# Layer modulation of a two-layer diffusion trunk: contraction summed on VectorE, partitions summed on TensorE, one block of 512 columns at a time

## The chip, the core and the metric

The kernel is one program on one core of one Trainium2 chip. The metric is device time in microseconds (us). The engines are named as in the profile: PE is TensorE, PEld its weight loads, DVE is VectorE, ACT is ScalarE, POOL is GpSimd, and SP issues the DMAs. Each engine works through its own instructions in a fixed order.

## The reference, cut to what matters

The model is a trunk of two layers with 512 latent and 256 context tokens and width 1024. In each layer the token mixer and the ConvFFN are modulated by six vectors (shift, scale, gate, twice), which come from a conditioning vector for each stream:

```python
silu_c, silu_cc = jax.nn.silu(c), jax.nn.silu(c_ctx)          # 1 x 1024 each
mod_x = split(silu_c  @ ada_w[l] + ada_b[l], 6)               # ada_w[l]: 1024 x 6144, latent stream
mod_c = split(silu_cc @ ada_w[l] + ada_b[l], 6)               # context stream
o_ctx, o_lat = token_mixer(modulate(h_ctx, mod_c[0], mod_c[1]), modulate(h_lat, mod_x[0], mod_x[1]), ...)
new_lat = post_norm(h_lat, mod_x[2] * o_lat, ...)
f_lat   = conv_ffn(modulate(new_lat, mod_x[3], mod_x[4]), ...)
new_lat = post_norm(new_lat, mod_x[5] * f_lat, ...)
```

The token mixer has four branches (retention, latent attention, SSD, LRU). Each branch's output is multiplied by its branch matrix, weighted by the sigmoid of a gate projection, and the four are summed.

## The kernel before, in words

All fp32 products are made of three matmuls on a high and a low part (lines 220 to 222 are such a triple). A weight tile of 128x1024 arrives by DMA from SP into `wr`; ACT rounds it to `wh` (line 205), and DVE makes the remainder `wl` in two subtractions of 128x512 (line 143, called from line 209). These three are rings of a few slots.

In each layer the mixer is one long chain, written branch by branch, and behind it a queue of *merge units* (the function `merge`), 8 for each branch, 32 in a layer. A unit multiplies a gate column (24 matmuls on the 512 latent tokens and, in layer 0, 24 on the 256 context tokens) and a branch column (12 and 12). ACT takes the tanh of the gate (line 1442), and DVE multiplies with the branch product: `s<-s,g` of 128x512, then of 128x256 (both by the helper on line 152). A unit after the first branch adds the earlier sum, a 128x768 or two smaller additions on line 143. The function `weave` places these units between the steps of the chain: each step of the chain brings a credit, each unit says by its `yield` what credit it uses up, and units are drawn while there is credit. So a unit is PE work that fills the places where the chain would leave PE idle. A scheduler then fixes the order of each engine's instructions before the run, by the order of writing, by raised priorities (weights are brought forward) and by its own estimates.

Each modulation vector is two blocks of 512 columns, so there are 12 blocks in a layer. The four that the first layer's start needs are made ahead. The other 20 are made by the generator `ada_all` in five groups of four blocks: 20 steps, one behind each of the first 20 merge units of layer 0. A step loads four tiles of 512 KB of `ada_w`, straight into `wh` and `wl` slots. Eight matmuls (line 349) have 32 columns of the conditioning vector `silu` as weights, and write 32 rows each, so that four blocks stand side by side in one PSUM tile `g`. ACT or DVE (lines 351, 353) then adds that to the group's sum `r`. At the end of a group that needs column vectors (three of the five; `MODV`) four matmuls with `sel` (line 358) turn them, and the helper `ada_col` adds the bias on DVE into `modc`. The other two groups load the bias by DMA (line 366), add it, and store rows to DRAM (line 370).

Of the kernel before, what the change touches and what calls it, by code (L numbers as in the profile page):

```python
# [8 lines left out]
F32 = mybir.dt.float32  # L9
# [7 lines left out]
P = 128  # L17
# [51 lines left out]
ADA_R = 'hlhl'  # L69
# [29 lines left out]
def trunk(tc, xin, cc, const, pv, pr, rows, ada_b, ada_w, w_in, w_uq, w_ukv, w_lg, w_br, w_out, w_up, w_dn, out):  # L99
# [3 lines left out]
    def nm(p):  # L103
        uid[0] += 1
        return f"{p}{uid[0]}"
# [3 lines left out]
    with ExitStack() as ctx:  # L109
        E = ctx.enter_context  # L110
        cp = E(tc.tile_pool(name="cp", bufs=1))
# [6 lines left out]
        dp = E(tc.tile_pool(name="dp", bufs=1, space=DRAM))  # L118
# [3 lines left out]
        act, dve, pool, pe, sy = nc.scalar, nc.vector, nc.gpsimd, nc.tensor, nc.sync  # L122

        def S(dt=F32, w=T):
            return cur[-1].tile([P, w], dt, tag="q" if w == 512 and len(cur) == 2 else "s", name=nm("s"), **({"bufs": N_HALF} if w == 512 and len(cur) == 2 else {}))

        def G():
            return pg.tile([P, 512], F32, tag="g", name=nm("g"))

        def C():  # L130
            return pc.tile([P, 512], F32, tag="c", name=nm("c"))

        def small(n, tag="sm", dt=F32):
            return sm.tile([P, n], dt, tag=tag, name=nm(tag))

        def T256(dt=F32, tag="t"):
            return tp.tile([P, 256], dt, tag=tag, name=nm("t"), bufs=N_T if tag == "t" else N_V)
# [4 lines left out]
        def tt(o, a, b, op):  # L142
            dve.tensor_tensor(out=o, in0=a, in1=b, op=op)  # L143

        def ts(o, a, s1, op0, s2=None, op1=None):
            if s2 is None:
                dve.tensor_scalar(out=o, in0=a, scalar1=s1, scalar2=None, op0=op0)
            else:
                dve.tensor_scalar(out=o, in0=a, scalar1=s1, scalar2=s2, op0=op0, op1=op1)

        def stt(o, a, s, b, op0, op1, total=None):
            dve.scalar_tensor_tensor(out=o, in0=a, scalar=s, in1=b, op0=op0, op1=op1, accum_out=total)  # L152

        MUL, ADD, SUB, MAX, MIN = ALU.mult, ALU.add, ALU.subtract, ALU.max, ALU.min
# [38 lines left out]
        def W4(tag, n, dt=F32R):  # L193
            return wp.tile([P, 1024], dt, tag=tag, name=nm(tag), bufs=n)

        def whole(ap, f=1024, tag="wr"):
            t = W4(tag, {"wr": N_WR, "wh": N_WH, "wl": N_WL}[tag], F32)
            sy.dma_start(out=t[:, 0:f], in_=ap[:, 0:f])
            return t
# [110 lines left out]
        modr = [dp.tile([2, 2, 2, 512], F32, name=f"modr{l}") for l in range(DEPTH)]  # L310
        sel = cp.tile([P, 10], F32, name="sel")
        sy.dma_start(out=sel, in_=const[:, _CO["sel"][0]:_CO["sel"][0] + 10])
        MODV = {0: 0, 1: 1, 3: 2, 4: 3}
# [13 lines left out]
        def ada_col(l, b, src, n):  # L327

            vec, half = b // 2, b % 2
            c0 = 16 + 32 * l + 8 * MODV[vec] + 4 * half  # L330
            stt(modc[l][:, MODV[vec], :, 4 * half:4 * half + 4 * n], src, float(vec in (1, 4)), cct[:, c0:c0 + 4 * n].rearrange("p (s j) -> p s j", s=1).to_broadcast([P, 2, 4 * n]), ADD, ADD)

        def ada_store(l, b, r):
# [3 lines left out]
                pe.matmul(p2[:, 2 * j:2 * j + 2], lhsT=r[:, j * P:(j + 1) * P], rhs=sel[:, 0:2], start=j == 0, stop=j == 3, skip_group_check=True)  # L337
            ada_col(l, b, p2[:, 0:8].rearrange("p (j s) -> p s j", s=2), 1)

        def ada_all(groups):  # L340

            for l, bs in groups:
                r = S(w=512)
                for u in range(4):
                    ws = [whole(ada_w[l, b, u], tag="w" + ADA_R[j]) for j, b in enumerate(bs)]
                    ps = G()
                    for k in range(2):
                        for j in range(4):
                            pe.matmul(ps[32 * j:32 * j + 32, :], lhsT=silu[:, 8 * u + 4 * k:8 * u + 4 * k + 32], rhs=ws[j][:, 512 * k:512 * k + 512], start=k == 0, stop=k == 1, skip_group_check=True)  # L349
                    if u == 0:  # L350
                        act.copy(r, ps)
                    else:
                        tt(r, r, ps, ADD)
                    yield
                if bs[0] // 2 in MODV:
                    p2 = C()
                    for q in range(4):
                        pe.matmul(p2[:, 8 * q:8 * q + 8], lhsT=r[:, q * P:(q + 1) * P], rhs=sel[:, 2:10], start=q == 0, stop=q == 3, skip_group_check=True)
                    p4 = p2[:, 0:32].rearrange("p (q j s) -> p j s q", q=4, j=4)
                    for j, b in enumerate(bs):  # L360
                        ada_col(l, b, p4[:, j], 1)
                else:
                    for h in range(2):
                        b2 = T256()
                        for j, b in enumerate(bs):
                            sy.dma_start(out=b2[32 * j:32 * j + 32, :], in_=ada_b[l:l + 1, b * 512 + 256 * h:b * 512 + 256 * (h + 1)].to_broadcast([32, 256]))
                        tt(r[:, 256 * h:256 * (h + 1)], r[:, 256 * h:256 * (h + 1)], b2, ADD)
                    ts(r[0:64, :], r[0:64, :], 0.5, MUL)
                    for j, b in enumerate(bs):
                        sy.dma_start(out=modr[l][j // 2, :, j % 2, :], in_=r[32 * j:32 * j + 2, :])  # L370

        def drain(g, n=10 ** 9):
            for _ in range(n):
                if next(g, "end") == "end":
                    return
# [1051 lines left out]
        def merge(WG, WB, hT, bo, acc, first, last, full):  # L1427

            allsl = slice(0 if full else CTX, T)
            segs = [SEG_L] + ([SEG_C] if full else [])  # L1430
            bw = None
            for f in range(8):
                wh, wl = unit(WG(f), shape=(8, 128))
                gp = fm(wh, wl, 8, hT, segs)
                if f % 2 == 0:
                    bw = unit(WB(f // 2), shape=(8, 128))
                o = 4 * (f % 2)
                bp = fm(bw[0][:, o:o + 4, :], bw[1][:, o:o + 4, :], 4, bo, segs)
                t = S()
                for (p, off, n), (b, _, _) in zip(gp, bp):  # L1440
                    sl = slice(off, off + n)
                    act.activation(out=t[:, sl], in_=p[:, 0:n], func=AF.Tanh, scale=0.5)
                    stt(t[:, sl], t[:, sl], 1.0, b[:, 0:n], ADD, MUL)
                if first:
                    acc.append(dp.tile([P, T], F32, name=nm("acc")))
                else:
                    r = S()
                    sy.dma_start(out=r[:, allsl], in_=acc[f][:, allsl])
                    tt(t[:, allsl], t[:, allsl], r[:, allsl], ADD)
                if last:  # L1450
                    acc[f] = t
                else:
                    sy.dma_start(out=acc[f][:, allsl], in_=t[:, allsl])
                yield (11.7 if full else 7.8) + (3.5 if next(ada_rest, 1) is None else 0)


        def phase(n):
# [23 lines left out]
        silu = cp.tile([P, 60], F32, name="silu")  # L1481
# [28 lines left out]
        ada_rest = ada_all([(0, rows_), (0, cols_), (1, (0, 1, 2, 3)), (1, rows_), (1, cols_)])  # L1510

        for l in range(DEPTH):
            full = l < DEPTH - 1
# [13 lines left out]
            acc = []  # L1527
# [3 lines left out]
            def weave(gen):  # L1531

                while True:
                    c = next(gen, None)
                    if c is None:
                        break
                    credit[0] += c
                    while fill and credit[0] > 0:
                        with earlier(O_FILL):
                            d = next(fill[0], None)  # L1540
                        if d is None:
                            fill.pop(0)
                        else:
                            credit[0] -= d
                    if not fill:
                        credit[0] = min(credit[0], 0.0)
# [4 lines left out]
            ro, mo, so, lo_, lat, kr = [], [], [], [], {}, []  # L1551
# [13 lines left out]
            weave(lru(prep, W, lambda u: w_lg[l, u], hT, full, lo_))  # L1565
            queue(2, lo_, last=True)
            weave(iter([1e9]))

            bc = load_bc(l, 0)
            hT2 = new_hT()  # L1570
# [19 lines left out]
            for p in pairs:  # L1590
# [6 lines left out]
                ps = tm_wide(lambda k: plain_unit(w_out[l, k]) if k in plain else unit(w_out[l, k]), 8, lambda k: plain_pair(acc[k], p) if k in plain else pair_of(acc[k], p), STAG[0][l])  # L1597
# [50 lines left out]
            for p in pairs:  # L1648
# [7 lines left out]
                ps = tm_wide(lambda k: unit(w_dn[l, k]), NF, lambda k: pair_of(sv[k], p, not full and p == pairs[-1]), STAG[1 if p != pairs[-1] else 2][l])  # L1656
                w = PW[1 + (p == pairs[-1])][l]
# [162 lines left out]
```

## Time and profile before

| | |
|---|---|
| median of three runs | 2853.22 us (2852.99 to 2856.61) |
| profiled execution | 2853.17 us |
| span of its trace | 2851.4 us |
| PE busy | 2797.8 us, 98% |
| DVE busy | 1859.2 us, 65% |
| ACT busy | 1254.1 us, 44% |
| DMA, mean | 128 GB/s |

The profiled execution is the one that all rows come from; 1.8 us of it lie outside the span. Busy time counts overlapping matmuls once. An engine's idle time is put down to the instruction that released it, in brackets in the timelines. Tile names are cut of their numbers, so `g` is any PSUM tile of that pool and `s` any SBUF tile.

### The profile page before, as it was taken

How to read it: one execution, taken by the hardware profiler on the slowest of the kernel's cores; microseconds unless marked ns; L12 is line 12 of the kernel's file. 1: busy time of each engine (PE TensorE's matmuls, PEld its weight loads, DVE VectorE, ACT ScalarE, POOL GpSimd, SP SyncE). 2: the span in 40 equal slices, each digit the busy share in tenths (PEclk: the TensorE clock that was granted, in tenths of full speed). 3: DMA queues.
4: the chain of work that ended last, by engine and by line, in shares of the span. 5: the costliest groups of instructions: out<-in, count | busy, mean ns of one | idle time of the engine just before them, and what ended most of it. 6: DMA issues, size and time to landing. Idle time of an engine off the chain costs nothing.

```text
span 2851.4 us, 40284 instructions
## 1 busy us (share of the span) xinstructions
PE 2797.8 (98%) x15248; PEld 2365.0 (83%) x15248; DVE 1859.2 (65%) x4005; ACT 1254.1 (44%) x2291; POOL 51.9 (2%) x70
## 2 busy tenths in 40 slices
PE   8999999999999999999999999999999999899998
PEld 5988879888888886888888778888888888688887
DVE  6554438777576448755557876555887685876667
ACT  4323235434455325533335653244554673453353
POOL 0000000000000000000000000000000000000000
PEclk9999999999999999999999999999999999999999
DMA  7212441445343345412125663121134334542265
GB/s 259 69 48 89 168 156 38 146 173 192 122 168 118 108 155 193 133 60 67 60 80 197 211 214 93 51 98 60 46 112 136 104 113 150 200 148 96 96 202 174
DMA packets 129169, 363.65 MB, mean 128 GB/s; under 512 B 14368, under 2 KB 29600, under 8 KB 128976
## 3 DMA queue, kind: packets, MB, share of 16 engines
q1 hardware_dynamic: 128976, 361.09, 37.7%
q8 instruction: 120, 1.97, 0.3%
q14 instruction: 73, 0.60, 0.1%
HBM read 332.59 MB, written 26.35 MB: 126 GB/s over the span
## 4 chain that ended last, share of the span: by engine, by line
PE 85%; DVE 7%; DMA 2%; ACT 2%; issue 1%; POOL 1%; SPq 0%; DVEq 0%; POOLq 0%; ACTq 0%
PE g L220 18%; PE g L221 18%; PE g L222 18%; PE g L581 3%; PE g L584 3%; PE g L585 3%; PE g L282 3%; PE g L283 2%; PE g L284 2%; DVE o L152 1%; DVE wl L143 1%; PE g L349 1%; PE g L252 1%; PE g L251 1%; PE g L250 1%
## 5 line engine op out<-in xcount | busy, mean ns | idle before, releaser
L143 DVE TENSOR_TENSOR wl<-wr,wh 128x512 fp32r<-128x512 f32 (+1 forms) x866 | 567.6, 683 | 429.6 <-ACT wh L205 396.7
L220 PE MATMUL g<-hh,wh 128*128 128x512 f32 (+1 forms) x2384 | 843.0, 354 | 0.8 <-DVE s L152 0.8
L221 PE MATMUL g<-hl,wh 128*128 128x512 f32 (+1 forms) x2384 | 838.2, 352 | 0.0
L222 PE MATMUL g<-hh,wl 128*128 128x512 f32 (+1 forms) x2384 | 837.5, 351 | 0.0
L205 ACT CAST wh<-wr 128x1024 fp32r<-128x1024 f32 x405 | 422.9, 1046 | 504.8 <-PE g L221 298.1
L220 PEld LDWEIGHTS g<-hh,wh 128*128 128x128 f32 x2384 | 451.5, 189 | 66.4 <-issue 6.6
L222 PEld LDWEIGHTS g<-hh,wl 128*128 128x128 f32 x2384 | 451.1, 189 | 58.2
L221 PEld LDWEIGHTS g<-hl,wh 128*128 128x128 f32 x2384 | 451.5, 189 | 57.0
L143 DVE TENSOR_TENSOR s<-s,s 128x256 f32<-128x256 f32 (+4 forms) x332 | 206.9, 645 | 26.4 <-ACT s L1183 14.7
L584 PE MATMUL g<-wh,t 128*128 128x512 f32 x468 | 183.7, 393 | 2.0 <-DVE t L143 1.8
L581 PE MATMUL g<-wh,t 128*128 128x512 f32 x468 | 184.6, 395 | 0.0
L585 PE MATMUL g<-wl,t 128*128 128x512 f32 x468 | 182.4, 390 | 0.0
L221 PE MATMUL g<-s,wh 128*128 128x512 f32 (+1 forms) x452 | 160.7, 356 | 0.0
L220 PE MATMUL g<-s,wh 128*128 128x512 f32 (+1 forms) x452 | 160.4, 355 | 0.0
L222 PE MATMUL g<-s,wl 128*128 128x512 f32 (+1 forms) x452 | 160.0, 354 | 0.0
L152 DVE SCALAR_TENSOR_TENSOR s<-g,pv,s 128x511 f32<-128x511 f32 (+2 forms) x176 | 111.6, 642 | 61.8 <-ACT s L605 59.9
L152 DVE SCALAR_TENSOR_TENSOR s<-s,s 128x512 f32<-128x512 f32 (+2 forms) x130 | 98.2, 756 | 54.3 <-ACT s L1630 26.9
L152 DVE SCALAR_TENSOR_TENSOR s<-s,g 128x512 f32<-128x512 f32 x118 | 70.6, 603 | 91.5 <-PE g L222 57.9
L282 PE MATMUL g<-wh,hh 128*128 128x512 f32 (+1 forms) x320 | 124.3, 389 | 0.8 <-ACT s L724 0.8
L283 PE MATMUL g<-wh,hl 128*128 128x512 f32 (+1 forms) x320 | 124.3, 388 | 0.0
L284 PE MATMUL g<-wl,hh 128*128 128x512 f32 (+1 forms) x320 | 123.5, 386 | 0.0
L152 DVE SCALAR_TENSOR_TENSOR s<-g,fcg,s 128x511 f32<-128x511 f32 (+1 forms) x128 | 83.9, 655 | 52.0 <-ACT s L605 50.1
(307 smaller groups left out, 4360.6 us busy)
## 6 DMA issues: line engine op xcount, KB each, us to landing
wr<-in_w_in_dram SPq DMA_DIRECT2D x120, 512.0 KB, 3.5
wr<-in_w_dn_dram SPq DMA_DIRECT2D x110, 512.0 KB, 4.3
wr<-in_w_up_dram SPq DMA_DIRECT2D x100, 512.0 KB, 3.5
wh<-in_ada_w_dram SPq DMA_DIRECT2D x46, 512.0 KB, 3.8
wl<-in_ada_w_dram SPq DMA_DIRECT2D x46, 512.0 KB, 5.1
wr<-in_w_out_dram SPq DMA_DIRECT2D x40, 512.0 KB, 3.5
wr<-in_w_br_dram SPq DMA_DIRECT2D x32, 512.0 KB, 3.5
wr<-in_w_in_dram SPq DMA_DIRECT2D x48, 256.0 KB, 3.0
```

The costliest lines, as they stand in the source:

```text
L143: dve.tensor_tensor(out=o, in0=a, in1=b, op=op)
L152: dve.scalar_tensor_tensor(out=o, in0=a, scalar=s, in1=b, op0=op0, op1=op1, accum_out=total)
L205: act.copy(hi[:, 0:f], raw[:, 0:f])
L220: pe.matmul(o, lhsT=sh, rhs=mh, start=start, stop=False)
L221: pe.matmul(o, lhsT=sh, rhs=ml, start=False, stop=False)
L222: pe.matmul(o, lhsT=sl, rhs=mh, start=False, stop=stop)
L282: pe.matmul(o[:, 0:w], lhsT=sh, rhs=wkh, start=k == 0, stop=False)
L283: pe.matmul(o[:, 0:w], lhsT=sl, rhs=wkh, start=False, stop=False)
L284: pe.matmul(o[:, 0:w], lhsT=sh, rhs=wkl, start=False, stop=k == len(ws) - 1)
L581: pe.matmul(ps[a][h], lhsT=xh, rhs=wh[:, cs], start=k == 0, stop=wl is None and k == nk - 1)
L584: pe.matmul(ps[a][h], lhsT=xl, rhs=wh[:, cs], start=False, stop=False)
L585: pe.matmul(ps[a][h], lhsT=xh, rhs=wl[:, cs], start=False, stop=k == nk - 1)
```

## The change

In the changed kernel a block is contracted on DVE. For each of the block's four weight tiles (two in `wl`, two in `wh`) DVE takes each half (128x512) twice, once multiplied by the latent column of `silu`, which is one number in each partition, and once by the context column, and adds it to `lat` or `con`. That is 16 DVE instructions a block, two `tensor_scalar` and 14 `scalar_tensor_tensor` (both by helpers, the latter on line 152). Four matmuls with a 128x32 tile of ones as weights (line 362) then sum `lat` and `con` over the partitions, in halves of 256 columns. For blocks that need column vectors, ACT copies the sum, two DMAs store it as a line to DRAM, and a third reads it back with partition and column exchanged, for `ada_col`. For the others the bias comes by four DMAs, is added on DVE, and two DMAs store the rows.

A whole block stands behind every second merge unit in layer 0 (16 blocks), and behind every fourth in layer 1 (the last four). The credit of a unit is 11.9 in layer 0 and 8.0 in layer 1, where it was 11.7 and 7.8, with 3.5 more where a step stood behind it. Lines behind the change have higher numbers by 12 to 16.

```diff
--- before.py
+++ after.py
@@ -337,37 +337,49 @@
                 pe.matmul(p2[:, 2 * j:2 * j + 2], lhsT=r[:, j * P:(j + 1) * P], rhs=sel[:, 0:2], start=j == 0, stop=j == 3, skip_group_check=True)
             ada_col(l, b, p2[:, 0:8].rearrange("p (j s) -> p s j", s=2), 1)
 
+        ones = cp.tile([P, 32], F32, name="ones")
+        dve.memset(ones, 1.0)
+
         def ada_all(groups):
 
             for l, bs in groups:
-                r = S(w=512)
-                for u in range(4):
-                    ws = [whole(ada_w[l, b, u], tag="w" + ADA_R[j]) for j, b in enumerate(bs)]
+                for j, b in enumerate(bs):
+                    lat, con = S(w=512), S(w=512)
+                    for u in range(4):
+                        w = whole(ada_w[l, b, u], tag="wh" if u % 2 else "wl")
+                        for k in (2 * u, 2 * u + 1):
+                            x = w[:, k % 2 * 512:(k % 2 + 1) * 512]
+                            c0, c1 = silu[:, 4 * k:4 * k + 1], silu[:, 4 * k + 1:4 * k + 2]
+                            for acc, c in ((lat, c0), (con, c1)):
+                                if k == 0:
+                                    ts(acc, x, c, MUL)
+                                else:
+                                    stt(acc, x, c, acc, MUL, ADD)
                     ps = G()
-                    for k in range(2):
-                        for j in range(4):
-                            pe.matmul(ps[32 * j:32 * j + 32, :], lhsT=silu[:, 8 * u + 4 * k:8 * u + 4 * k + 32], rhs=ws[j][:, 512 * k:512 * k + 512], start=k == 0, stop=k == 1, skip_group_check=True)
-                    if u == 0:
-                        act.copy(r, ps)
+                    for s, x in enumerate((lat, con)):
+                        for h in range(2):
+                            q = 64 * s + 32 * h
+                            pe.matmul(ps[q:q + 32, 0:256], lhsT=ones, rhs=x[:, 256 * h:256 * h + 256], start=True, stop=True, skip_group_check=True)
+                    r = T256()
+                    if b // 2 in MODV:
+                        act.copy(r, ps[:, 0:256])
+                        line = dp.tile([2, 512], F32, name=nm("line"))
+                        dst = [line[s] for s in range(2)]
                     else:
-                        tt(r, r, ps, ADD)
+                        b2 = T256()
+                        for q in range(4):
+                            sy.dma_start(out=b2[32 * q:32 * q + 32, :], in_=ada_b[l:l + 1, b * 512 + 256 * (q % 2):b * 512 + 256 * (q % 2 + 1)].to_broadcast([32, 256]))
+                        tt(r, ps[:, 0:256], b2, ADD)
+                        if j < 2:
+                            ts(r, r, 0.5, MUL)
+                        dst = [modr[l][j // 2, s, j % 2, :] for s in range(2)]
+                    for s in range(2):
+                        sy.dma_start(out=dst[s].rearrange("(h c) -> h c", h=2), in_=r[64 * s:64 * s + 64:32, :])
+                    if b // 2 in MODV:
+                        p2 = small(8, "p2").rearrange("p (s q) -> p s q", s=2)
+                        sy.dma_start(out=p2, in_=line.rearrange("s (q p) -> p s q", p=P))
+                        ada_col(l, b, p2, 1)
                     yield
-                if bs[0] // 2 in MODV:
-                    p2 = C()
-                    for q in range(4):
-                        pe.matmul(p2[:, 8 * q:8 * q + 8], lhsT=r[:, q * P:(q + 1) * P], rhs=sel[:, 2:10], start=q == 0, stop=q == 3, skip_group_check=True)
-                    p4 = p2[:, 0:32].rearrange("p (q j s) -> p j s q", q=4, j=4)
-                    for j, b in enumerate(bs):
-                        ada_col(l, b, p4[:, j], 1)
-                else:
-                    for h in range(2):
-                        b2 = T256()
-                        for j, b in enumerate(bs):
-                            sy.dma_start(out=b2[32 * j:32 * j + 32, :], in_=ada_b[l:l + 1, b * 512 + 256 * h:b * 512 + 256 * (h + 1)].to_broadcast([32, 256]))
-                        tt(r[:, 256 * h:256 * (h + 1)], r[:, 256 * h:256 * (h + 1)], b2, ADD)
-                    ts(r[0:64, :], r[0:64, :], 0.5, MUL)
-                    for j, b in enumerate(bs):
-                        sy.dma_start(out=modr[l][j // 2, :, j % 2, :], in_=r[32 * j:32 * j + 2, :])
 
         def drain(g, n=10 ** 9):
             for _ in range(n):
@@ -1451,7 +1463,9 @@
                     acc[f] = t
                 else:
                     sy.dma_start(out=acc[f][:, allsl], in_=t[:, allsl])
-                yield (11.7 if full else 7.8) + (3.5 if next(ada_rest, 1) is None else 0)
+                if f % 2 == 0 if full else f % 4 == 0:
+                    drain(ada_rest, 1)
+                yield 11.9 if full else 8.0
 
 
         def phase(n):
@@ -1565,6 +1579,8 @@
             weave(lru(prep, W, lambda u: w_lg[l, u], hT, full, lo_))
             queue(2, lo_, last=True)
             weave(iter([1e9]))
+            if not full:
+                drain(ada_rest)
 
             bc = load_bc(l, 0)
             hT2 = new_hT()
```

The first place is PE at one merge unit of the first branch in layer 0. Before, the eight matmuls of a step stand behind the last product of a merge unit (`g_3522` is the branch product of the context), the first four of them shown:

```order
L221 MATMUL g_3522<-s_2089,wh_3504 128x256
L222 MATMUL g_3522<-s_2088,wl_3506 128x256
L349 MATMUL g_3568<-wh_3560,silu 32x512
L349 MATMUL g_3568<-wl_3562,silu 32x512
L349 MATMUL g_3568<-wh_3564,silu 32x512
L349 MATMUL g_3568<-wl_3566,silu 32x512
```

After, the four matmuls on `ones` stand there (the program has the sums `s_3553` and `s_3554`, which are `lat` and `con` of a block), and then the next unit's first gate product:

```order
L221 MATMUL g_3533<-s_2091,wh_3515 128x256
L222 MATMUL g_3533<-s_2090,wl_3517 128x256
L362 MATMUL g_3579<-s_3553,ones 32x256 x2
L362 MATMUL g_3579<-s_3554,ones 32x256 x2
L220 MATMUL g_3600<-hh_98,wh_3595 128x512
L221 MATMUL g_3600<-hl_99,wh_3595 128x512
```

What moved: the matmuls that read weight tiles are replaced by ones that read two sums of DVE, at the same place in PE's order, ahead of the next unit.

The second place is DVE at the same unit. Before, the two evictions of the unit stand alone between the weight subtractions of units to come:

```order
L143 TENSOR_TENSOR wl_3582<-wr_3578,wh_3580 128x512 x2
L152 SCALAR_TENSOR_TENSOR s_3535<-s_3535,g_3509 128x512
L152 SCALAR_TENSOR_TENSOR s_3535<-s_3535,g_3522 128x256
L143 TENSOR_TENSOR wl_3690<-wr_3686,wh_3688 128x512 x2
L143 TENSOR_TENSOR wl_3747<-wr_3743,wh_3745 128x512 x2
```

After, the block's sums stand around them (`g_3520` and `g_3533` are the unit's products):

```order
L152 SCALAR_TENSOR_TENSOR s_3546<-s_3546,g_3520 128x512
L152 SCALAR_TENSOR_TENSOR s_3553<-wl_3567,silu,s_3553 128x512
L152 SCALAR_TENSOR_TENSOR s_3546<-s_3546,g_3533 128x256
L152 SCALAR_TENSOR_TENSOR s_3554<-wl_3567,silu,s_3554 128x512
L152 SCALAR_TENSOR_TENSOR s_3553<-wh_3573,silu,s_3553 128x512
L152 SCALAR_TENSOR_TENSOR s_3554<-wh_3573,silu,s_3554 128x512
L152 SCALAR_TENSOR_TENSOR s_3553<-wh_3573,silu,s_3553 128x512
L152 SCALAR_TENSOR_TENSOR s_3554<-wh_3573,silu,s_3554 128x512
L143 TENSOR_TENSOR wl_3687<-wr_3683,wh_3685 128x512 x2
```

What moved: five of the block's sums now stand behind the eviction of `g_3533`, the last product ahead of the `ones` matmuls.

The third place is DVE at a later unit, in the LRU branch, after the change (`s_8961` and `s_8962` are a block's sums, `s_8952` the unit's result, `g_8939` its last product):

```order
L152 SCALAR_TENSOR_TENSOR s_8952<-s_8952,g_8939 128x256
L152 SCALAR_TENSOR_TENSOR s_8961<-wh_8969,silu,s_8961 128x512
L143 TENSOR_TENSOR s_8952<-s_8952,s_8957 128x768
L152 SCALAR_TENSOR_TENSOR s_8962<-wh_8969,silu,s_8962 128x512
L152 SCALAR_TENSOR_TENSOR s_8961<-wl_8975,silu,s_8961 128x512
L152 SCALAR_TENSOR_TENSOR s_8962<-wl_8975,silu,s_8962 128x512
L152 SCALAR_TENSOR_TENSOR s_8961<-wl_8975,silu,s_8961 128x512
L152 SCALAR_TENSOR_TENSOR s_8962<-wl_8975,silu,s_8962 128x512
L152 SCALAR_TENSOR_TENSOR s_8961<-wh_8981,silu,s_8961 128x512
L152 SCALAR_TENSOR_TENSOR s_8962<-wh_8981,silu,s_8962 128x512
L152 SCALAR_TENSOR_TENSOR s_8961<-wh_8981,silu,s_8961 128x512
L152 SCALAR_TENSOR_TENSOR s_8962<-wh_8981,silu,s_8962 128x512
```

What moved: here ten sums and the addition of the unit's earlier sum stand behind the eviction, where before only that addition stood behind it.

## Rows read from the trace of the kernel before

**Rows 1.** The page, busy time by engine, share of the span, instructions.

```profile
PE 2797.8 (98%) x15248; PEld 2365.0 (83%) x15248; DVE 1859.2 (65%) x4005; ACT 1254.1 (44%) x2291; POOL 51.9 (2%) x70
```

**Rows 2.** The page, chain that ended last, shares of the span.

```profile
PE 85%; DVE 7%; DMA 2%; ACT 2%; issue 1%; POOL 1%; SPq 0%; DVEq 0%; POOLq 0%; ACTq 0%
```

**Rows 3.** Windows: start:end, length, busy by engine (count), granted clock, DMA share, GB/s.

```profile
270.00:545.00 275.00, 271.05 (x1754) 231.83 (x1753) 159.53 (x408) 107.78 (x254) 2.27 (x1) 1.00 0.34 119
545.00:1045.00 500.00, 499.40 (x2912) 423.39 (x2911) 308.96 (x583) 224.04 (x383) 1.32 (x1) 1.00 0.43 149
...
1880.00:2205.00 325.00, 321.19 (x1779) 276.38 (x1778) 239.07 (x590) 154.63 (x346) 3.28 (x2) 1.00 0.28 91
```

**Rows 4.** Window of the whole span, line 349 alone: PE and weight loads.

```profile
0.00:2851.00 2851.00, 38.49 (x320) 8.37 (x320) 1.00 0.38 128
```

**Rows 5.** The same window, line 358 alone.

```profile
0.00:2851.00 2851.00, 2.87 (x24) 2.95 (x24) 1.00 0.38 128
```

**Rows 6.** Timeline of PE, 360 us: start, duration, line, tiles, form.

```profile
348.08 0.50 PE L220 MATMUL g<-hh,wh 128*128 128x512 f32 x1
...
360.58 0.28 PE L222 MATMUL g<-s,wl 128*128 128x256 f32 x1
360.79 0.62 PE L349 MATMUL g<-wh,silu 128*32 128x512 f32 x1
...
362.64 0.50 PE L220 MATMUL g<-hh,wh 128*128 128x512 f32 x1
```

**Rows 7.** Timeline of DVE around it; in brackets idle before and its releaser.

```profile
359.47 0.69 DVE L152 SCALAR_TENSOR_TENSOR s<-s,g 128x512 f32<-128x512 f32 x1 [2.70 <-PE g L222]
360.97 0.42 DVE L152 SCALAR_TENSOR_TENSOR s<-s,g 128x256 f32<-128x256 f32 x1 [0.81 <-PE g L222]
```

**Rows 8.** Timeline of DVE in a full stretch at 2785 us.

```profile
2784.65 1.28 DVE L143 TENSOR_TENSOR wl<-wr,wh 128x512 fp32r<-128x512 f32 x2
2785.86 1.29 DVE L152 SCALAR_TENSOR_TENSOR o<-s,o 128x512 f32<-128x512 f32 x2
...
2790.79 1.40 DVE L152 SCALAR_TENSOR_TENSOR o<-o,mv,s 128x512 f32<-128x512 f32 x2
2792.11 1.41 DVE L152 SCALAR_TENSOR_TENSOR o<-o,rs,s 128x512 f32<-128x512 f32 x2
```

**Rows 9.** Groups by form, DVE: count, busy, mean ns, idle before.

```profile
L143 DVE TENSOR_TENSOR s<-s,s 128x768 f32<-128x768 f32 x64 | 60.8, 956 | 15.6 <-ACT s L1183 14.7
...
L152 DVE SCALAR_TENSOR_TENSOR o<-o,mv,s 128x512 f32<-128x512 f32 x32 | 23.0, 745 | 1.0 <-ACT t L399 1.0
...
L152 DVE SCALAR_TENSOR_TENSOR s<-s,g 128x256 f32<-128x256 f32 x36 | 15.0, 418 | 17.6 <-PE g L222 17.6
```

**Rows 10.** Timeline of DVE in the last LRU column of layer 0.

```profile
929.36 0.96 DVE L143 TENSOR_TENSOR s<-s 128x768 f32<-128x768 f32 x1 [6.04 <-ACT s L1178]
...
944.75 0.95 DVE L143 TENSOR_TENSOR s<-s,s 128x768 fp32r<-128x768 f32 x1
```

**Rows 11.** DMA issues: KB each, median us to landing.

```profile
acc<-s SPq DMA_DIRECT2D x24, 256.0 KB, 2.3
...
t<-in_ada_b_dram SPq DMA_DIRECT2D x16, 32.0 KB, 1.8
```

**Rows 12.** Windows where the granted clock fell and did not (last: PE only).

```profile
2460.00:2470.00 10.00, 8.25 (x34) 5.05 (x35) 8.03 (x19) 8.28 (x16) 0.68 (x2) 1.00 0.90 314
...
2480.00:2490.00 10.00, 6.05 (x37) 5.49 (x35) 9.12 (x22) 5.35 (x7) 1.67 (x2) 0.83 0.40 137
...
2485.70:2488.00 2.30, 2.29 (x10) 0.50 0.32 55
```

**Rows 13.** Timeline of PE before the fall: waits in brackets.

```profile
2482.50 0.39 PE L1580 MATMUL c<-hh,wh 128*128 128x256 f32 x1 [1.24 <-ACT wh L205]
...
2485.71 0.58 PE L1582 MATMUL g<-hh,wl 128*128 128x256 f32 x1 [2.71 <-DVE wl L143]
```

**Rows 14.** Timeline of PE, the wait inside the other window.

```profile
2461.23 0.44 PE L420 MATMUL c<-cst,s 128*128 128x128 f32 x2 [1.95 <-ACT s L441]
```

## The prediction, made before the changed kernel ran

> **What bounds the kernel now.** I read the page's busy times first: PE is busy 2797.8 of 2851.4 us, DVE 65% of the span, ACT 44% [rows 1]. The chain that ended last agrees: 85% of it lies on PE, 7% on DVE [rows 2]. Then the windows of the stretches in which blocks will stand. In layer 0 PE is busy 271.05 of 275 us (270 to 545) and 499.40 of 500 (545 to 1045), at a granted clock of 1.00; in layer 1, 321.19 of 325 (1880 to 2205) [rows 3]. So only 3.95 + 0.6 + 3.81 = 8.4 us of PE idle time there could take something up. PE work saved is time saved, and every us for which PE waits is nearly a us lost. DVE has room on average; what counts is where its work stands.
>
> **What goes.** Line 349 has 320 matmuls, yet they occupy only 38.49 us of PE: four column groups run at once [rows 4]. One step shows it, with its first matmul at 360.79 and the next unit's product at 362.64, 1.85 us for 16 records [rows 6]. The 24 records of `sel` are 2.87 us [rows 5]. So 41.4 us of PE go, and no more. On DVE the additions of the steps go, beside PE work: nothing.
>
> **What comes on PE.** Four matmuls of 256 columns a block. The nearest rows: a product of 128x256 whose successor starts about 0.21 later [rows 6], and a step's 16 records of 512 columns in 1.85. I take 0.6 a block, 12 us for 20; between 5 (side by side) and 20.
>
> **What comes as waiting, the main term.** PE takes its work in order. The `ones` matmuls stand directly behind a merge unit's last product, and ahead of the next unit. On DVE, a part of the block's 16 sums stands behind the eviction of that last product. The eviction can't run before PE has finished the product; then DVE does the sums behind it; PE meanwhile stands before `ones` with nothing allowed past it. DVE's idle time earlier, as the 2.70 and 0.81 us around one unit [rows 7], does not help those sums.
>
> In the new order I counted the sums behind the last eviction, block by block: 11, 9, 5, 5, 4, 14, 13, 12, 14, 7, 11, 10, 13, 5, 5, 5, 13, 14, 11, 13: 194 of 320. Price of one: the trace has no sum of this form (fp32, 128x512, one number in each partition) on its own, but two of `o<-o,mv,s` are followed after 1.32 us, so 0.66 each; below it stands a plain subtraction, two in 1.21, so 0.605 [rows 8], above it that form's single duration of 745 ns [rows 9]. I take 0.66, the spacing in a full DVE, and keep 0.605 and 0.75.
>
> - 194 sums at 0.66: 128 us.
> - What else stands in these tails: 12 additions of 128x768 at 0.87 (956 ns alone [rows 9], less the 0.08 by which the spacing of the 512 form is under its duration), 10.4; two additions of 512 and seven subtractions at 0.6, 5.4.
> - The handing over, 20 times: the last product starts at 360.58 and its eviction at 360.97 [rows 6, 7]. With some 0.12 for the product itself (an estimate, under the 0.21 to the next start) that is 0.27; the eviction 0.36 (418 ns alone [rows 9]); and some 0.2, an estimate from the 0.27, until PE learns of the last sum. 0.8 each, 16 us.
> - In four blocks PE has work of its own between product and `ones`: minus 10.
>
> That is 150 us: 4 to 5 us for six blocks, 7 to 12 for the rest. By the bounds of a sum 139 to 167. Of the 8.4 us of idle time that PE has there, half may be absorbed: minus 4.
>
> **Filler.** Each unit used to pay 15.2 of credit with a step and 11.7 without: 20 x 15.2 + 12 x 11.7 = 444. Now all 32 pay 11.9: 381. So units are drawn earlier, and in the last LRU column of layer 0 the order has none left that doesn't need its output. That column's chain on DVE and ACT runs from 929.36 to past 944.75, some 16 us without its projection [rows 10], in which PE was filled. With the projection I put it at 20, against some 11 us of PE work of its own: 10 us lost, 0 if the waits ahead have let DVE catch up, 20 with nothing beside it.
>
> **The clock.** In the window of 2480 to 2490 the granted clock is 0.83: after PE waits of 1.24 and 2.71 us close together it is 0.50, the lower level of 1.2 GHz, and matmuls of 256 columns take 0.58 for 0.28 [rows 12, 13]. 0.83 over 10 us is 3.4 us at half speed, so 1.7 us of work lost. In the window with one wait of 1.95 us it stays at 1.00 [rows 12, 14]. Of the new waits 13 are of 7 us or more; I let these pay 1.7: 22 us. If none pays, 0; if all 20, 34. The Trainium skill ("TensorE: Matmul & The Clock Gate", section "HAM oscillation — how this bites in real kernels") says that PE's clock is throttled after idling, and that a kernel which waits between bursts pays the slow start after every wait. The row at 0.50 agrees, the one at 1.00 after a wait does not; were all 20 waits to pay, the term would be 34 and the sum 3019.
>
> **Column vectors.** For 12 blocks `ada_col` waits on DVE for ACT's copy, two stores and a load from DRAM. Rows near it land in 2.3 (store) and 1.8 us (a small load) [rows 11], so with the copy the chain is some 5.5. In the order DVE has 1.2 to 8.1 us of other work before `ada_col`; behind it wait the weight subtractions of coming units, whose units are some 12.7 us of products away (a unit runs from 348.08 to 360.79 [rows 6]). That cover hides most of it: 5 us for all, between 0 and 30. The Trainium skill ("DMA: Bandwidth & Descriptors", "Rules for kernel authors") says that a strided last dimension becomes one descriptor per element; this load is of that kind (1024 elements of 4 bytes), and no row of before shows such a one, so by the page it lands later than the 1.8 of the row, which is the way of the third rival. The stores stand on SP too, ahead of weight loads, and wait for ACT; weights are loaded early enough that I put that at nothing, and its failure is the rival below.
>
> **Sum.** Against the profiled execution, 2853.17 (span 2851.4 and 1.8 around it, 0.05 under the median): 2853.2 - 41.4 + 12 + 150 - 4 + 10 + 22 + 5 = 3006.8. I forecast 3007 us, 5.4% slower.
>
> **Rivals.**
> - *The sums are hidden.* If DVE has its sums done when PE comes to `ones`, the change is 2853 - 41 + 12 = 2824, faster. It decides only where the tail behind the eviction is under about 1.5 us (29 us saved over 20 blocks). For it: DVE is idle 35% [rows 1], and idle around the units [rows 7]. Against: the idle time lies ahead of the eviction, and the tail behind it, in a fixed order; the shortest tail is four sums, 2.6 us. 0.04; and 0.02 for ending by chance within 0.2% (5.7 us, what a measurement here can tell from no change).
> - *The waits, but no clock and no lost filler.* The array keeps its clock as in rows 14, and the last LRU column finds its inputs ready. 2853 - 41 + 12 + 150 - 8 + 0 + 0 = 2966, or 2955 at 0.605 a sum. For it: DVE waits may run shorter than 7 us. Against: 13 waits longer than any in rows 13. 0.20.
> - *`ada_col` and SP hold the rest.* DVE stands at `ada_col` for the load, weights come late, and PE waits a second time in each of the 12 blocks: 12 x 4 to 5 = 55 in place of 5, 3057. For it: every later `wl` is behind it on DVE. Against: 12.7 us of products as cover. 0.14.
> - *As forecast*, 2975 to 3045: 0.60.
>
> **The numbers.** Low end: all bounds on the low side, 2853 - 41 + 5 + 139 - 8 = 2948; I take 2945. High end: 2853 - 41 + 20 + 167 + 20 + 34 + 5 = 3058; with half of the third rival, 3075. Under 2945 is mostly the first rival, above 3075 the worst of the third. Faster 0.04, same 0.02, slower 0.94.
>
> **What would show it.** In the profile after: PE idle before line 362 released by DVE's line 152, 130 to 165 us in all, longest waits 10 to 12; PE busy near 2770 less what a lower clock adds; DVE busy 200 us more (320 x some 0.65); a granted clock under 1.00 just behind the long waits and 1.00 elsewhere; line 349's 38 us gone. Wrong would be: PE reaching `ones` with no wait, or the loss standing before units' first products, released by `wl` (the third rival), or a clock of 1.00 throughout (the second).

## The result and the profile after

The changed kernel takes 3037.03 us (median of 4 runs, 3034.97 to 3038.69), against 2854.23 us for the kernel before, run beside it: a ratio of 1.0641, with a 95% interval of 1.0628 to 1.0654. The prediction was 3007 us within 2945 to 3075. The profiled execution is one of 3038.69 us, with a span of 3036.9.

The page after, busy times by engine, answers to [rows 1], and the first line of the chain that ended last to [rows 2]:

```profile
PE 2828.4 (93%) x15064; PEld 2388.1 (79%) x15064; DVE 2050.8 (68%) x4317; ACT 1258.4 (41%) x2298; POOL 52.3 (2%) x70
...
PE 68%; DVE 12%; ACT 3%; issue 2%; DMA 2%; POOL 1%; SPq 0%; DVEq 0%; POOLq 0%; ACTq 0%
```

PE has 184 fewer instructions, and yet it is busy 30.6 us longer; and it is idle 208.5 us, where 53.6 were. Two things happened, then: PE waits, and its work takes longer. The waits of PE, largest first (engine, line and tile that waited, what released it: us in total, times, longest):

```profile
PE g L362 <- DVE s L152: 133.8, 19, 12.2
PE g L220 <- ACT s L216: 11.2, 1, 11.2
PE g L362 <- ACT s L1361: 6.2, 1, 6.2
```

All 20 blocks are there: 19 waits before the `ones` matmuls end with a sum of DVE; the one put down to ScalarE ends at 736.30 us, 0.14 behind a sum of its block as well. The second row is the last LRU column. Together they are 151.2 of the 154.9 us of new idle time. One block, on DVE and then on PE (timelines after; start, duration, line, tiles; in brackets the idle time before and its releaser):

```profile
373.53 0.69 DVE L152 SCALAR_TENSOR_TENSOR s<-s,g 128x512 f32<-128x512 f32 x1 [2.82 <-PE g L222]
374.14 0.75 DVE L152 SCALAR_TENSOR_TENSOR s<-wl,silu,s 128x512 f32<-128x512 f32 x1
374.96 0.42 DVE L152 SCALAR_TENSOR_TENSOR s<-s,g 128x256 f32<-128x256 f32 x1
375.30 0.75 DVE L152 SCALAR_TENSOR_TENSOR s<-wl,silu,s 128x512 f32<-128x512 f32 x1
375.96 2.73 DVE L152 SCALAR_TENSOR_TENSOR s<-wh,silu,s 128x512 f32<-128x512 f32 x4
```

```profile
378.18 1.33 PE L362 MATMUL g<-s,ones 128*32 128x256 f32 x8 [3.33 <-DVE s L152]
379.44 0.80 PE L220 MATMUL g<-hh,wh 128*128 128x512 f32 x1
```

This is the second place of the order shown ahead: behind the eviction of 128x256 come five sums. Ahead of the eviction DVE had stood idle for 2.82 us. Four sums take 2.73 us, three starts at 0.66 and one whole duration of 0.75. So the last sum ends at 378.69, but PE goes on at 378.18: the first two `ones` matmuls read `lat` alone, whose last sum is the next to last of all and ends at 378.03. The other waits whose ends I compare (286.29, 345.99, 2091.36 us) end in the same place, 0.14 to 0.15 us behind the next to last sum.

The second loss is the clock. The same PE from 282 us on, around the first block (its wait is 7.21 us and ends at 286.29), in windows of 2 us (start and end, length, busy time and count, granted clock, DMA share, GB/s):

```profile
282.00:284.00 2.00, 0.00 (x0) 0.88 0.00 0
284.00:286.00 2.00, 0.00 (x0) 0.50 0.00 0
286.00:288.00 2.00, 1.71 (x9) 0.50 0.00 0
288.00:290.00 2.00, 2.00 (x9) 0.50 0.00 0
290.00:292.00 2.00, 2.00 (x16) 0.91 0.01 2
```

The clock falls to 0.50 (1.2 GHz) while PE still waits, and comes back only after some 4.1 us of work (0.91 over the last window is 0.36 us of it at 0.50). I took such windows of 1 us over the whole span and summed PE's busy time times what the clock lacks of 1.00: 59.8 us after, 6.7 before. Behind each of the 20 waits between 1.5 and 3.1 us are lost, behind the shortest (3.33 us) too, 47 together. The LRU column's wait has 1.3 behind it (the next wait comes 2.6 us later), 6.7 are as much as the kernel before lost, and 4.7 lie in other places. The third effect is small: the `ones` matmuls are 32.65 us of PE, most of it at the lower clock; with the clock up for most of them the same matmuls took 15.83 (the first experiment below).

The sum from the traces: 2853.2 - 41.4 + 15.8 for `ones` + 140.0 of waits + 11.2 for the LRU column + 53.1 of clock + 3.7 of other idle time = 3035.6; 3.1 us of the measured 3038.7 are in no term.

### The profile page after: what moved, and what is told of

It is laid out like the page before. It is cut to its first block, busy times and chain, and to the rows that moved or that the text cites. A ratio compares the mean times of both kernels' runs of the same rounds, so it can differ in the third digit from the quotient of the medians.

```text
span 3036.9 us, 40299 instructions
## 1 busy us (share of the span) xinstructions
PE 2828.4 (93%) x15064; PEld 2388.1 (79%) x15064; DVE 2050.8 (68%) x4317; ACT 1258.4 (41%) x2298; POOL 52.3 (2%) x70
## 3 DMA queue, kind: packets, MB, share of 16 engines
q8 instruction: 119, 1.95, 0.3%
## 4 chain that ended last, share of the span: by engine, by line
PE 68%; DVE 12%; ACT 3%; issue 2%; DMA 2%; POOL 1%; SPq 0%; DVEq 0%; POOLq 0%; ACTq 0%
PE g L220 15%; PE g L221 15%; PE g L222 15%; DVE s L152 5%; PE g L593 3%; PE g L596 3%; PE g L597 3%; DVE s L143 2%; PE g L282 2%; PE g L284 2%; PE g L283 2%; DVE wl L143 1%; DVE o L152 1%; PE g L362 1%; PE c L220 1%
## 5 line engine op out<-in xcount | busy, mean ns | idle before, releaser
L220 PE MATMUL g<-hh,wh 128*128 128x512 f32 (+1 forms) x2384 | 856.6, 359 | 1.8 <-DVE s L152 1.1
L221 PE MATMUL g<-hl,wh 128*128 128x512 f32 (+1 forms) x2384 | 849.0, 356 | 0.0
L222 PE MATMUL g<-hh,wl 128*128 128x512 f32 (+1 forms) x2384 | 847.6, 356 | 0.0
L220 PEld LDWEIGHTS g<-hh,wh 128*128 128x128 f32 x2384 | 459.8, 193 | 78.4 <-issue 16.9
L221 PEld LDWEIGHTS g<-hl,wh 128*128 128x128 f32 x2384 | 460.1, 193 | 58.7
L222 PEld LDWEIGHTS g<-hh,wl 128*128 128x128 f32 x2384 | 458.4, 192 | 59.9
L143 DVE TENSOR_TENSOR s<-s,s 128x256 f32<-128x256 f32 (+5 forms) x332 | 207.4, 645 | 33.6 <-ACT s L1195 14.9
L220 PE MATMUL g<-s,wh 128*128 128x512 f32 (+1 forms) x452 | 160.5, 356 | 11.2 <-ACT s L216 11.2
L362 PE MATMUL g<-s,ones 128*32 128x256 f32 x160 | 32.6, 616 | 140.0 <-DVE s L152 133.8
L362 PEld LDWEIGHTS g<-s,ones 128*32 128x32 f32 x160 | 7.9, 137 | 152.4 <-issue 122.0
```

Source lines behind the costliest of these rows:

```text
L220: pe.matmul(o, lhsT=sh, rhs=mh, start=start, stop=False)
L221: pe.matmul(o, lhsT=sh, rhs=ml, start=False, stop=False)
L222: pe.matmul(o, lhsT=sl, rhs=mh, start=False, stop=stop)
L362: pe.matmul(ps[q:q + 32, 0:256], lhsT=ones, rhs=x[:, 256 * h:256 * h + 256], start=True, stop=True, skip_group_check=True)
```

## The experiments

"Before" runs beside each set at 2853.0 to 2853.8 us. Each kernel is the changed one with the edit shown.

**The `ones` matmuls one unit later.** The generator pauses between the sums and the `ones` matmuls, and each half is drawn behind a unit of its own:

```diff
                                     stt(acc, x, c, acc, MUL, ADD)
+                    yield
                     ps = G()
...
-                if f % 2 == 0 if full else f % 4 == 0:
+                if full or f % 4 < 2:
                     drain(ada_rest, 1)
```

> The four ones matmuls of a block and what follows them stand one merge unit later; the sums on VectorE are the same 320. Theory (the order: PE waits because sums stand behind the eviction of the product that the ones matmuls follow): in the new order no sum stands behind that eviction, so the 140 us of waits before the ones matmuls fall under 10, the clock loss of 53 us falls under 10, and the time is 2853 - 41 + 15 + 11 for the last LRU column = 2838 us, between 2825 and 2855. Rival (the load: 320 more instructions on VectorE delay the weights, wherever they stand): the waits move to the units' first products, and the time stays above 2950.

Measured: 2879.75 us (ratio to before 1.0091, 1.0074 to 1.0108). The waits of PE and the `ones` line alone over the whole span (PE and weight loads, clock):

```profile
PE g L220 <- ACT s L216: 11.2, 1, 11.2
PE g L363 <- DVE s L152: 9.0, 3, 4.1
```

```profile
0.00:2877.00 2877.00, 15.83 (x160) 3.72 (x160) 0.99 0.37 127
```

The waits before `ones` went from 140 to 9 and the clock's loss from 59.8 to 18.5, with the same 320 sums on DVE (busy 2043.8 us). So the waits belonged to where the sums stand, close ahead of `ones`; the same number of them a unit ahead leaves 9 us of these waits. But the time is 25 us over the top of the range expected. The timeline of PE shows where: in layer 1.

```profile
1822.00 0.30 PE L836 MATMUL c<-cst,t 128*128 128x128 f32 x1 [0.45 <-DVE t L149]
...
1887.75 0.95 PE L363 MATMUL g<-s,ones 128*32 128x256 f32 x4 [3.75 <-DVE s L152]
...
1945.12 0.63 PE L363 MATMUL g<-s,ones 128*32 128x256 f32 x4 [4.06 <-DVE s L152]
...
2128.62 0.47 PE L220 MATMUL g<-hh,wh 128*128 128x512 f32 x1 [2.94 <-DVE s L152]
...
2512.18 0.39 PE L1599 MATMUL g<-hh,wl 128*128 128x256 f32 x1 [2.80 <-DVE wl L143]
```

From the first to the last of these rows are 690.2 us. In the kernel before, the same two instructions lie 655.7 us apart (2485.71 of [rows 13] less the 1830.00 of this row):

```profile
1830.00 0.30 PE L823 MATMUL c<-cst,t 128*128 128x128 f32 x1 [0.44 <-DVE t L149]
```

Four blocks in layer 1 thus cost 34.5 us, over 8 a block; before, that layer had none. 19.5 of them are more idle time of PE (30.3 us, where 10.8 were), 6.8 are lost to the clock, which stood at 1.00 there before. Up to the first of these instructions the kernel is 8 us faster.

**The sums ahead of the eviction.** The `ones` matmuls stay directly behind the unit, and the sums get a raised priority, so that no sum stands behind the last eviction (`O_SUM` is 60):

```diff
+                    with tc.high_priority(offset=O_SUM):
-                    for u in range(4):
+                        for u in range(4):
...
```

> The ones matmuls stay directly behind the unit's last product, as in the changed kernel; the block's loads and sums get a raised priority, so that all 16 stand ahead of the last eviction in VectorE's order. Theory (the order): the same as with the ones matmuls one unit later, 2838 us, between 2825 and 2860, waits before the ones matmuls under 15 us. Rival (the distance: the ones matmuls need a whole unit between the sums and themselves, whatever the order of the eviction): waits of 2 us or more stay in most blocks, the clock falls there, and the time is 2900 or more.

Measured: 2972.09 us (1.0414, 1.0398 to 1.0429). The rival held, and my theory, as it stood, did not. The waits before `ones` are 80.1 us in 14 places by DVE. One of them, first on DVE, then on PE (the helper's line is 153 here, `ones` 364):

```profile
331.33 0.49 DVE L148 TENSOR_SCALAR s<-wl,silu 128x512 f32<-128x512 f32 x1 [0.86 <-PE c L1033]
...
342.01 2.73 DVE L153 SCALAR_TENSOR_TENSOR s<-wh,silu,s 128x512 f32<-128x512 f32 x4
344.78 1.02 DVE L153 SCALAR_TENSOR_TENSOR s<-s,g 128x512 f32<-128x512 f32 x2
```

```profile
338.33 0.28 PE L223 MATMUL g<-s,wl 128*128 128x256 f32 x1
344.23 1.64 PE L364 MATMUL g<-s,ones 128*32 128x256 f32 x8 [5.62 <-DVE s L153]
```

The sums are ahead of both evictions now, and PE still stands: from the first sum at 331.33 until DVE is through they take 13.4 us with other work of DVE between them, and PE had come 5.6 us before it could go on. So a tail behind the eviction is enough for the waits, as in the changed kernel, but they come without it too. I read the need behind it as wider: a block asks for 11 to 13 us of DVE, and PE must have as much to do between the block's first sum and its `ones`. One unit, 12.7 us [rows 6], is about that much. No run varies this distance in small steps.

**Half of the sums.** All positions stay, the context stream is summed over a single half tile:

```diff
-                            for acc, c in ((lat, c0), (con, c1)):
+                            for acc, c in ((lat, c0), (con, c1))[:1 if k else 2]:
```

> The changed kernel with the context sums left out but for the first of each block: 9 sums a block in place of 16, so the context stream's modulation is not the reference's. All positions stay; 73 sums stand behind the evictions that were 194. Theory (each sum behind the eviction is 0.66 us of PE waiting): the waits before the ones matmuls fall from 140 to 75 or 80, the clock loss by a third, and the time is near 2946, between 2920 and 2970. Rival (the waits come from the position of the ones matmuls and the chains behind them, hardly from the sums): above 3000.

Measured: 2981.92 us (1.0449, 1.0434 to 1.0465), 55 us under the changed kernel, but above the range expected; the waits are 92.9 us, not 75 to 80:

```profile
PE g L362 <- DVE s L152: 92.9, 19, 8.9
```

The direction is the theory's: fewer sums behind the eviction, less waiting (140 to 93). The size isn't. I had counted sums alone; in the new order more of DVE's other work stands between them (seven other instructions in the tail of the sixth block). The clock's loss is 44.1 us, for only some of the waits became short.

**No round trip to DRAM.** A constant in place of the column vectors:

```diff
-                        line = dp.tile([2, 512], F32, name=nm("line"))
...
-                        p2 = small(8, "p2").rearrange("p (s q) -> p s q", s=2)
-                        sy.dma_start(out=p2, in_=line.rearrange("s (q p) -> p s q", p=P))
-                        ada_col(l, b, p2, 1)
+                        ada_col(l, b, nhalf[:, 0:8].rearrange("p (s q) -> p s q", s=2), 1)
```

> Leaves out the stores of the 12 column blocks' sums to DRAM and the loads that turn them; a constant stands in place of the column vectors. All else is the changed kernel. Theory (the order): the round trip lies beside PE work, VectorE's 21 us of waiting for it cost nothing, and the time is 3030 to 3040 us. Rival (the round trip holds VectorE and with it the weights): 2985 to 3015.

Measured: 3038.6 us (1.0644, 1.0628 to 1.066), the time of the changed kernel within its spread. DVE did wait for the trip (first row, changed kernel, DVE's waits), and PE's waits without it are the same (second row):

```profile
DVE modc L152 <- DMA p<-line: 20.9, 5, 6.1
```

```profile
PE g L362 <- DVE s L152: 134.2, 19, 12.2
```

So 20.9 us of waiting on DVE cost nothing at the end. The third rival of the prediction is out.

**Credit.** The `ones` matmuls a unit later, with `yield 13.9` in place of 11.9 in layer 0.

> The ones matmuls one merge unit later, and 13.9 in place of 11.9 of credit for a unit in layer 0, which is the sum that the 32 units of the kernel before used up (444). Theory (filler): units are left for the last LRU column, the wait of 11 us there goes with some 3 us of lower clock, and the time is 12 to 14 us under that with the ones late alone, near 2825. Rival (the column's wait is only moved to another place with too little filler): within 5 us of the ones late alone.

Measured: 2884.01 us (1.0105, 1.0089 to 1.012): the rival. The LRU column's wait is gone, and others have come, 13.4 us before `ones` for ACT's tanh:

```profile
PE g L363 <- ACT s L1455: 13.4, 5, 5.1
```

I read this as units that follow each other with nothing between, where the `ones` result wants one of the four PSUM buffers from which a unit's gates and products are read; the runs with the other pool below bear on it, but no run changes that alone.

**Halves, all in layer 0.** Eight sums behind each unit of layer 0, a block's `ones` behind the first half of the next block, its result in the other PSUM pool (`finish` holds the `ones` matmuls, with `ps = C()`, and what follows them); no block in layer 1:

```diff
+                        if late and u == 1:
+                            finish(*late)
+                        if u % 2:
+                            yield
+                    late = (l, j, b, lat, con)
...
-                if f % 2 == 0 if full else f % 4 == 0:
-                    drain(ada_rest, 1)
+                if full:
+                    drain(ada_rest, 1 + (f % 4 == 3) + (f == 7))
```

> All 20 blocks in layer 0, as in the kernel before; 8 sums of a block behind each merge unit in place of 16 behind every second, a block's ones matmuls behind the first half of the next block's sums, one unit or more later, and their result in a PSUM buffer of the other pool (c). Theory (VectorE's sums cost where a lump of them stands between two things PE needs, and layer 1 has no room for it): the 34 us that layer 1 lost with the ones late alone go to under 5, 11 to 14 us for the last LRU column stay, and the time is 2853 - 41 + 13 + 14 + 7 (ten sums still behind an eviction) = 2846 us, between 2835 and 2855. Rival (320 sums more on VectorE cost some 25 us wherever they stand): 2870 to 2885.

Measured: 2870.76 us (1.0058, 1.0043 to 1.0073), which is the rival's range. Layer 1's loss is gone (1845.30 to 2503.33 between the same two instructions, 658.0 us); layer 0 ends 15.3 us later than before. 11.2 us of PE's waiting there are the LRU column's; another part is seen at 400 us, behind a unit with three halves, where the sums keep DVE until 405.8 and PE then waits for a weight (DVE, then PE):

```profile
401.00 0.87 DVE L147 TENSOR_SCALAR s<-wl,silu 128x512 f32<-128x512 f32 x2
401.79 1.41 DVE L152 SCALAR_TENSOR_TENSOR s<-wl,silu,s 128x512 f32<-128x512 f32 x2
403.12 2.73 DVE L152 SCALAR_TENSOR_TENSOR s<-wh,silu,s 128x512 f32<-128x512 f32 x4
405.77 1.61 DVE L143 TENSOR_TENSOR wl<-g,s 128x512 fp32r<-128x512 f32 x3
```

```profile
406.51 0.58 PE L250 MATMUL g<-wh,s 128*128 128x256 f32 x1 [4.74 <-DVE wl L143]
```

The pool alone, `ps = G()` in the same kernel:

> The halves with 11.9 of credit, and the ones matmuls' result in a buffer of the units' own pool (g), as in the changed kernel. Theory (the pool matters only where units stand back to back): 0 to 10 us over the same with the other pool. Rival (the pool decides what is left of the loss): 15 us or more over it.

2880.08 us (1.0092, 1.0076 to 1.0109): 9.3 us more, in the theory's range. But the waits that grew before `ones` are again for sums of DVE, with `ps = C()` (first) and `ps = G()` (second), and none for ACT:

```profile
PE c L350 <- DVE s L152: 3.9, 3, 1.5
```

```profile
PE g L350 <- DVE s L152: 14.7, 3, 8.7
```

So this run does not show `ones` waiting for a buffer. The credit at 13.9, and then at 15.2 (all else as in the halves with the other pool):

> The same with 13.9 of credit for a unit in layer 0 in place of 11.9. Theory (with the ones late alone this credit only moved the wait of 11 us into ones matmuls that waited for a PSUM buffer of the units' own pool; in the other pool they do not wait): the LRU column's wait goes and nothing takes its place, 2830 us, between 2820 and 2840, faster than the kernel before by some 0.8%. Rival (the units left over at the end crowd VectorE and ScalarE there): within 5 us of the run with 11.9.

2861.91 us (1.0029, 1.0019 to 1.004): 9 us gained, where 16 were expected, so neither side has it; 6.1 us of the column's wait remained.

> The halves with the other PSUM pool and 15.2 of credit for a unit in layer 0. Theory (13.9 left 6.1 us of waiting in the last LRU column and 4 sums behind one eviction; more credit keeps more units for that column): the column's wait falls under 2 us, 8 to 10 us with the clock, and the time is 2852 to 2856, no different from the kernel before by more than 0.2%. Rival (what is gained there is lost at the end of the layer, where units then stand back to back): 2862 to 2870.

2850.98 us (0.9989, 0.9979 to 0.9999): the column's wait is gone, and nothing took its place. It is the fastest version, 2 us under the kernel before, less than 0.2%, and just under the range expected. Its page (of an execution of 2853.41 us) shows where the gain went that the two PE terms leave, 41.4 - 15.8 = 25.6 us:

```profile
PE 2778.0 (97%) x15064; PEld 2357.7 (83%) x15064; DVE 2041.0 (72%) x4317; ACT 1253.8 (44%) x2298; POOL 52.8 (2%) x70
```

PE is busy 19.8 us less than in [rows 1], in a span of 2851.6; so it is idle 20 us more, and that is where most of the gain went. Two last runs spread the halves in other ways, by the gate `1 + (f in (1, 4, 6))` with a credit of 16.2, and by two extra halves a branch and two more in the first with 15.2:

> The halves in the other PSUM pool, spread more evenly: never more than two halves behind one unit (three stood behind the last unit of a branch before), and 16.2 of credit. Theory (what is left is VectorE's sums crowding the next weights' subtractions, as the wait of 4.7 us at 404 us behind a unit with three halves): that wait goes with its lower clock, 5 to 8 us, and the time is 2840 to 2848, faster than the kernel before by 0.2% or more. Rival (some 20 us of small waits come with 190 us more of VectorE work wherever they stand): 2848 to 2856.

> The halves in the other PSUM pool with 15.2 of credit, extra halves behind units 2 and 5 of each branch and two more in the first. Theory (crowding): as with the even spread, 2840 to 2850. Rival (small waits come with the work): 2848 to 2856.

2865.37 us (1.0041, 1.0028 to 1.0055) and 2859.97 us (1.0023, 1.0013 to 1.0032). In the first, the wait at 404 us went as the theory had it, but the time lies above both ranges, and the second's above both as well; waits for `wl` appear in other places, as in the first of the two:

```profile
PE g L222 <- DVE wl L143: 6.5, 2, 5.1
```

Whether another spread would give back the 20 us stays open.

## Why the prediction was right, point by point

- **What goes and what comes on PE.** 41.4 us went. The `ones` matmuls are 15.8 us with the clock mostly up (13.95 in the fastest version), where I put 12 between 5 and 20.
- **The waits.** 150 us were forecast for the 20 blocks and 4 of them absorbed; 140.0 were measured. The price of a sum, 0.66 from two `o<-o,mv,s` in a row [rows 8], is what four sums in a row show. "4 to 5 us for six blocks, 7 to 12 for the rest" came out as 3.33 to 4.20 for six and 6.21 to 12.23 for fourteen. A tail of five sums, 4.1 us by the prices of the prediction, measured 3.33, 0.8 less: it took PE to wait for the last sum, but the next to last, 0.66 earlier, lets it go on. Over 20 blocks that is 13 us, and yet the term is only 6 too high; what made up for the rest is not broken down here.
- **Filler.** 10 us forecast, 11.2 measured, and it went when the units used up more credit.
- **Column vectors.** 5 us forecast; nothing, by the run without the round trip. It was the cover that was right: the trip itself is longer than the 5.5 us put down. The first column block's stores are issued at 569.89 us and its turned load at 572.00, and DVE, which stood for it, goes on at 578.42, 6.4 us after that issue; the row for a small load was 1.8.
- **The clock is the step that was mis-sized.** "Of the new waits 13 are of 7 us or more; I let these pay 1.7: 22 us", with 34 as the upper bound. In fact all 20 pay, also the ones of 3.33 us, and each pays 2.35 on average: 47 us. Of these 25 us more, 12 are the seven waits that I let pay nothing, 13 the price. I took 1.7 from one fall, behind waits of 1.24 and 2.71 us [rows 12 and 13]; the two waits of 3.33 us paid 1.7 too, most of the others more. With the LRU column and the other places the clock's term is 53 us, 31 more than forecast. That this is nearly the 30 us by which 3007 was short is in part luck: the misses of the other terms (waits 6 less, column vectors 5 less, `ones` 4 more, the LRU column 1 more, 7 of idle time and rest that had no term) cancel to about 1. The sentence by which the Trainium skill ("TensorE: Matmul & The Clock Gate", section "HAM oscillation — how this bites in real kernels") makes a kernel pay after every wait was nearer than my choice; I weighed it against one row, a wait of 1.95 us at a clock of 1.00, that was shorter than any of the new ones.
- **The range.** It held the time, but its upper end came from other terms. The clock's own bound, 34, was too low by 13 for the 20 waits alone, and by 19 in all.
- **The mechanism** held in the changed kernel: with the `ones` a unit later 131 of the 140 us of waits went. It was told too narrowly, as the run with the sums ahead of the eviction showed: the fixed order of the eviction is one way to start the sums late; what has to be covered, as I read the runs, is the lump of 11 to 13 us.

## What to carry to other kernels

When work is moved from the engine that bounds to one with time to spare, read the new order at the handing back: what the bounding engine asks for next must have been begun as long ago as the lump takes, with other work of the bounding engine in between. A busy share of 65% tells nothing on that. Price each new wait of TensorE with the slow clock behind it, here 1.5 to 3.1 us for each of the 20 waits, of 3.3 to 12.2 us, and note that a share of the saved work can turn into many small waits elsewhere: the best arrangement tried saved PE 20 us and ended within 0.2% of where it began.

## What the runs showed of the hardware that was not expected

The granted clock fell to 0.50 in the middle of a wait and stayed there for some 4.1 us of full work after the one at 286 us. It fell with a wait of 3.33 us too (at 378.18, windows of 2 us: the clock is 1.00 until 378 and falls only when the work has begun again):

```profile
376.00:378.00 2.00, 0.00 (x0) 1.00 0.51 197
378.00:380.00 2.00, 1.82 (x9) 0.78 0.19 37
380.00:382.00 2.00, 2.00 (x6) 0.50 0.88 299
382.00:384.00 2.00, 2.00 (x9) 0.87 1.02 397
```

So the shorter of the 20 waits lose almost as much as the long ones: 1.7 us behind this one, 2.33 behind the longest of 12.23. The clock fell behind shorter waits too: at 1242 us, where PE had just stood for 1.57 and 0.39 us, the granted clock of the changed kernel is 0.67 over 1242 to 1244 and 0.50 over the next 2 us, while before the change a wait of 1.95 us [rows 14] had no fall behind it.
